# A third token tile of full height, earlier FFN rows, another order of the first transfers, and a second norm with one power: a hybrid decoder layer on one core

## The chip, the core and the metric

The kernel runs on one core of one Trainium2 chip. A core has five engines that run side by side, each through its own instructions in order: TensorE (PE in the profile; PEld is its weight load) multiplies matrices into PSUM, VectorE (DVE) and ScalarE (ACT) do elementwise work, GpSimd (POOL) does small elementwise work and issues transfers, and SyncE (SP) issues transfers. Sixteen DMA engines move the data. Engines wait for each other by semaphores.

The metric is the device time of one launch in microseconds; lower is better. The profile is of one execution. Its times count from the start of the span, which is the time from the program's first instruction to its last.

## What is computed

One step of a decoder layer, on 256 prompt tokens (one sequence, states zero) and 64 sample tokens (8 sequences of 8 tokens, with states given). All 320 tokens go through the layer together; model width D = 2048.

```
u = x @ w_in                                  # q k v o i f z xbc dt: 4096 + 8 + 2560 + 16 columns
h_m = mlstm(q, k, v, o, i, f)                 # 4 heads of 256; matrix memory C, normaliser n, running max m
h_s = ssd(z, conv4(xbc), dt)                  # 16 heads of 64, state 64 x 128, two B/C groups
x = layer_norm1(2**0.25 * x + concat(h_m, h_s) @ w_out)
up = x @ w_up                                 # 2 x 5504 columns
c = conv3(up)                                 # depthwise over tokens; the two rows before come from state_ffn_conv
x = layer_norm2(2**0.25 * x + (silu(c_gate) * c_value) @ w_down)
```

`layer_norm` is (x - mean) * rsqrt(var + 1e-5) * g + b. The outputs are y for prompt and sample, and all new states. Everything is float32.

## The kernel before

**Layout.** Activations lie with features in the 128 partitions and the 320 tokens along the free axis: columns 0 to 255 are the prompt, 256 to 319 the sample. A big product is made as three matmuls on split operands: each weight and each activation is split into a rounded part `hi` (a ScalarE copy, L74) and a rest `lo` (a VectorE subtraction, L75), and hi x hi, hi x lo and lo x hi are added in PSUM. `run_groups` (L262) goes over output units of 128 features, in quarters of 4 k-tiles; each quarter is 12 matmuls of 320 columns. `Stream` loads the weights on SyncE's queue (the first two tiles on ScalarE's, L61) into four buffers of 512 KB and splits them four quarters ahead.

**Order.** The main stream is: w_in in 52 units, w_out in 16, then three rounds of w_up and w_down. Everything else is background work in generators (`Tasks`, L116). A task's `yield n` means: not again before the planner's clock has moved n ns. That clock is a sum of estimated matmul and transpose times (`mm`, `transpose`, L227 to 238), so it follows the order of PE's instructions and not real time. `run_groups` steps the tasks after each quarter (`pump`, L285). What a task emits takes its place in each engine's program order there. `wait(flag)` holds a task, not an engine; the engines wait only for data.

**Token tiles.** Where tokens must lie in partitions (a transpose, or a product that contracts over tokens) the kernel works in three tiles: tokens 0 to 127, 128 to 255, and the 64 sample tokens as a tile of 64 partitions (`tok`, L249). So many PE instructions are 64 rows high or 64 columns wide: the transposes of x (L410 to 412), of the mLSTM heads (L1253), the row broadcasts (`diag3`, `colbc`, L313 to 325), the scores and their products.

**The sample's state term.** For SSD and mLSTM the sample's output is a product with the step's own tokens plus a product with the old state. The state products of four sequences land in four 32-partition strips of one bank, 8 rows used in each (L833 and L1173). They are scaled into a tile `yi`, and a product with the selection matrix `sel` (L906 and L1227) takes the eight rows of each strip to the right tokens and adds them.

**First transfers** (L435 to 444, L392): SyncE issues x columns 0 to 255, the identity, the sample's first 512 columns, and then the rest; the first two weight tiles go out on ScalarE's queue. `x_transpose` (L402) makes `XH`, `XL` for 128 features from two prompt tiles and one sample tile. `load_small` (L462) issues some 17 small loads on GpSimd. `keep_x` (L416) adds XH and XL again for the gates.

**FFN rows.** `ffn_consts` (L1339) starts with the second w_out group; after `yield 25000` it issues ten loads of old conv rows and conv weights on GpSimd, after `yield 20000` more it transposes them on PE (L1350, L1356).

**The second norm.** `down_task` (L1530) adds the last product, transposes each 128 features to tokens-in-partitions and takes their statistics (`bn_stats`, L1549); `times_g` (L1558) multiplies them with g. After the last unit (L1618 to 1661) the 16 statistics are aggregated, the reciprocal root is made by a ScalarE root, a VectorE reciprocal and a refinement, the row terms are transposed, and 12 products of 5 rows bring b - mean * rs * g; VectorE (tiles 0 and 1) or ScalarE and GpSimd (the sample) add them, and SyncE stores.

Of the kernel before, what the change touches and what calls it, by code (L numbers as in the profile page):

```python
# [13 lines left out]
NT = 320  # L14
# [7 lines left out]
class Stream:  # L22
# [21 lines left out]
    def load(self, upto=None, own=()):  # L44

        own = list(own)
        while self.nr < len(self.raws) and (own or self.live < self.RB):
# [12 lines left out]
            for c in range(0, m, step):  # L60
                (self.nc.sync if self.nr > 1 else self.nc.scalar).dma_start(t[:, :, c:c + step], src[:, :, c:c + step])  # L61
# [109 lines left out]
def _hybrid_step(ctx, tc, I, O):  # L171
# [77 lines left out]
    def tok(i):  # L249
        return 128 if i < 2 else 64  # L250
# [3 lines left out]
    sel = cp.tile([128, 2, 64], F32, name="sel")  # L254
# [58 lines left out]
    def diag3(dg, cols_of):  # L313
        for i in range(3):
            n = tok(i)
            V.tensor_scalar(dg[0:n, i, 0:n], ident[0:n, 0:n], cols_of(i)[0:n], None, ALU.mult)
        return dg

    def colbc(dg):

        ps = bank()
        for i in range(3):
            n = tok(i)
            mm(ps[:, 128 * i:128 * i + n], ones[0:n, :], dg[0:n, i, 0:n], True, True)
        return ps
# [75 lines left out]

    def x_transpose(c, kks=range(4)):  # L402
# [4 lines left out]
        for kk in kks:  # L407
# [27 lines left out]
    xs_in = mt("T10", [64, D])  # L435
    for c in range(4):
        x_load(c)
        s = slice(512 * c, 512 * c + 512)
        dma(xs_in[:, s], I["x_sample"].rearrange("b t f -> (b t) f")[:, s])
        if c == 0:  # L440
            src = I["x_prompt"][0, :, 256:512].rearrange("(i p) f -> p i f", p=128)
            dma(box["x", 0][:, :, 256:512], src)
            own = [mt("T4", [128, 1024]) for _ in range(4)]
        st.load(2 * c + 2, (own[0:2], own[2:4], (), ())[c])
# [16 lines left out]

    def load_small():  # L462
# [14 lines left out]
        hr = mt("T10", [24, 1536])  # L477
        gdma(hr, I["state_ssm_conv"][0].rearrange("b r c -> (b r) c"))
        gdma(c_tm, I["c_tm"])
        gdma(dsk, I["ssm_D"].broadcast_to([128, 16]))  # L480
        gdma(m01, I["c_m01"])
        gdma(sel, I["c_sel"])
# [5 lines left out]
        for i in range(12):  # L488
            transpose(ps[:, 24 * i:24 * i + 24], hr[:, 128 * i:128 * i + 128])
        A.activation(histx, ps[:, 0:288].rearrange("p (a b) -> p a b", b=24), AF.Copy)  # L490
# [20 lines left out]
    def gate_task(pg):  # L511
        gf, gi = mt("T2", [128, 384]), mt("T2", [4, NT])
        V.memset(gf[:, NT:384], 0.0)
        V.tensor_copy(gf[:, 0:NT], pg[:, 0:NT])
# [5 lines left out]
        for i in range(3):  # L520
            mm(pt[:, 24 * i:24 * i + 24], gf[:, 128 * i:128 * i + 128], fold[:, 0:24], True, True)
        pf = bank()
        mm(pf[0:4, 0:NT], fold[:, 0:4], gf[:, 0:NT], True, True)
# [36 lines left out]
        transpose(pd[0:48, 0:64], dt3[0:64, 2, :])  # L560
# [4 lines left out]
        V.tensor_copy(dtf[32:48], pd[32:48, 0:64])  # L565
# [47 lines left out]
        for i in range(3):  # L613
            transpose(p1[:, 128 * i:128 * i + 128], T1[:, 128 * i:128 * i + 128])
        A.activation(TT1, p1[:, 0:384].rearrange("p (a b) -> p a b", b=128), AF.Copy)
        p2 = bank()
# [59 lines left out]
    def ssd_cb():  # L676
# [4 lines left out]
        for g in range(2):  # L681
# [3 lines left out]
            mm(ps[0:64, 384:448], B[:, g, 256:NT], C[:, g, 256:NT], True, True)  # L685
            t = mt("T2", [128, 448])
            G.memset(t[64:128, 384:448], 0.0)
            V.tensor_tensor(t[:, 0:384], ps[:, 0:384], m01[:, 0:384], ALU.mult)
            V.tensor_tensor(t[0:64, 384:448], ps[0:64, 384:448], m01[0:64, 384:448], ALU.mult)
# [76 lines left out]
    def ssd_xdt():  # L766
# [3 lines left out]
        for i in range(3):  # L770
            n = tok(i)
            for hh in range(2):
                ps = bank()
                for j in range(4):
                    transpose(ps[0:n, 128 * j:128 * j + 128], XS[:, 4 * hh + j, 128 * i:128 * i + n])
                V.tensor_tensor(by(xdt[0:n, i, 512 * hh:512 * hh + 512], 64), by(ps[0:n, :], 64),
                                bcl(dt3[0:n, i, 32 + 8 * hh:40 + 8 * hh], 64), ALU.mult)
                yield 500
        box["xdt"] = xdt
        flags.add("xdt")  # L780

    def ssd_sample():
# [22 lines left out]
        yield from wait("x4")  # L805
        yi = {}
        for b in range(8):
# [19 lines left out]
            if b % 4 == 3:  # L827
                x = b // 4
                for g in range(2):
# [6 lines left out]
                    yi[g, x] = y  # L836
# [5 lines left out]
        box["yi"] = yi  # L842
# [5 lines left out]
    def ssd_heads():  # L848
# [41 lines left out]
        for j in range(8):  # L890
# [47 lines left out]
    def ssd_norm():  # L938
        var = sm([128, 3, 2])
        G.memset(var, 1.0)  # L940
        for g in range(2):
# [10 lines left out]
            for i in range(3):  # L952
                mm(ps[0:tok(i), 2 * i:2 * i + 2], sq[:, 128 * i:128 * i + tok(i)], ones[:, 0:2], True, True)
            pv = ps[:, 0:6].rearrange("p (a b) -> p a b", b=2)
            V.tensor_scalar(var[:, 0:2, g], pv[:, 0:2, 0], 1.0 / 512, None, ALU.mult)
            V.tensor_scalar(var[0:64, 2:3, g], ps[0:64, 4:5], 1.0 / 512, None, ALU.mult)
# [769 lines left out]
```

## Time and profile before

| | |
|---|---|
| median of 3 runs | 1579.27 us (1578.6 to 1581.3) |
| the profiled execution | 1580.12 us, of it the span 1578.3 us |
| TensorE clock granted, mean over the execution | 0.992 |
| data moved by DMA | 253.97 MB, mean 161 GB/s |
| weight stream, first matmul | at 8.83 us |
| last output product to span's end | 1566.4 to 1578.3 us |

The page has the busy time of each engine, the span in 40 slices, the DMA queues, the chain of work that ended last, and groups of instructions. A group's row reads: line, engine, operation, out<-in, shape, xcount, then busy us and mean ns of one, then the idle time of the engine just before them. A row of the timeline reads: start and duration in us, engine, line, operation, out<-in, shape, count of instructions merged into it. `128*64` before a shape is the part of the array used: rows times columns. A PE product of float32 operands shows as two instructions. In the windows view a row has the stretch, its length, busy time and count of each engine (PE, PEld, DVE, ACT, POOL), the granted clock, the DMA engines' share and GB/s. PE's matmuls overlap, so the time that one takes is read from start to start.

### The profile page before, as it was taken

How to read it: one execution, taken by the hardware profiler on the slowest of the kernel's cores; microseconds unless marked ns; L12 is line 12 of the kernel's file. 1: busy time of each engine (PE TensorE's matmuls, PEld its weight loads, DVE VectorE, ACT ScalarE, POOL GpSimd, SP SyncE). 2: the span in 40 equal slices, each digit the busy share in tenths (PEclk: the TensorE clock that was granted, in tenths of full speed). 3: DMA queues.
4: the chain of work that ended last, by engine and by line, in shares of the span. 5: the costliest groups of instructions: out<-in, count | busy, mean ns of one | idle time of the engine just before them, and what ended most of it. 6: DMA issues, size and time to landing. Idle time of an engine off the chain costs nothing.

```text
span 1578.3 us, 27987 instructions
## 1 busy us (share of the span) xinstructions
PE 1553.8 (98%) x10547; PEld 1502.5 (95%) x10547; DVE 976.6 (62%) x1957; ACT 773.1 (49%) x1532; POOL 290.3 (18%) x601
## 2 busy tenths in 40 slices
PE   9999999999999997999999999999999999999997
PEld 7999999998889997999999999999999999999996
DVE  5775445656677585687777545565644465556765
ACT  3665433435445453476666435555533455555332
POOL 4213220024311073133321000000000000001301
PEclk9999999999999998999999999999999999999998
DMA  9456665577665566445554455455444545455642
GB/s 260 147 161 160 187 187 172 143 193 208 195 221 183 169 183 138 134 147 149 149 151 135 157 158 146 148 156 152 136 152 144 167 145 151 143 154 168 170 140 79
DMA packets 267080, 253.97 MB, mean 161 GB/s; under 512 B 18804, under 2 KB 261263, under 8 KB 266816
## 3 DMA queue, kind: packets, MB, share of 16 engines
q1 hardware_dynamic: 260432, 246.76, 53.2%
q0 software_dynamic: 4928, 4.37, 1.3%
q8 instruction: 82, 1.34, 0.3%
q10 hardware_dynamic: 1584, 1.05, 0.3%
q14 instruction: 54, 0.44, 0.1%
HBM read 231.63 MB, written 20.43 MB: 160 GB/s over the span
## 4 chain that ended last, share of the span: by engine, by line
PE 86%; issue 7%; DMA 2%; POOL 1%; DVE 1%; ACT 1%; POOLq 0%; SPq 0%; DVEq 0%; ACTq 0%
PE bk L232 84%; PE bk L238 2%; DMA rows<-ffn_conv_w 1%; POOL T L425 1%; DMA raw<-w_out 1%; DVE lo L75 1%; DMA T<-ln_g 0%; DMA gbias<-ssm_dt_bias 0%; DMA xT<-T 0%; POOL big L1654 0%; ACT hi L74 0%; DVE big L1393 0%; DVE big L1389 0%; ACT L657 0%; ACT T L644 0%
## 5 line engine op out<-in xcount | busy, mean ns | idle before, releaser
L75 DVE TENSOR_TENSOR lo<-raw,hi 128x512 fp32r<-128x512 f32 (+2 forms) x800 | 556.4, 706 | 391.7 <-ACT hi L74 389.3
L74 ACT ACTIVATE hi<-raw 128x512 fp32r<-128x512 f32 (+2 forms) x800 | 486.3, 616 | 455.9 <-PE bk L232 427.3
L232 PE MATMUL bk<-big,hi 128*128 128x320 f32 (+1 forms) x2752 | 609.3, 310 | 0.0
L232 PEld LDWEIGHTS bk<-big,hi 128*128 128x128 f32 x2752 | 462.2, 188 | 0.1
L232 PE MATMUL bk<-big,lo 128*128 128x320 f32 (+1 forms) x1376 | 426.5, 310 | 0.0
L232 PE MATMUL bk<-XH,hi 128*128 128x320 f32 x832 | 270.2, 325 | 0.1
L232 PEld LDWEIGHTS bk<-big,lo 128*128 128x128 f32 x1376 | 259.3, 188 | 0.0
L232 PE MATMUL bk<-XH,lo 128*128 128x320 f32 x832 | 258.2, 310 | 0.1
L232 PE MATMUL bk<-XL,hi 128*128 128x320 f32 x832 | 258.0, 310 | 0.0
L232 PE MATMUL bk<-HH,hi 128*128 128x320 f32 x688 | 214.2, 311 | 0.0
L232 PE MATMUL bk<-HH,lo 128*128 128x320 f32 x688 | 212.6, 309 | 0.0
L232 PE MATMUL bk<-HL,hi 128*128 128x320 f32 x688 | 212.5, 309 | 0.0
L232 PEld LDWEIGHTS bk<-XH,hi 128*128 128x128 f32 x832 | 157.2, 189 | 14.7 <-issue 5.5
L232 PEld LDWEIGHTS bk<-XL,hi 128*128 128x128 f32 x832 | 157.4, 189 | 0.4
L232 PEld LDWEIGHTS bk<-XH,lo 128*128 128x128 f32 x832 | 157.2, 189 | 0.6 <-DVE lo L75 0.6
L1492 DVE SCALAR_TENSOR_TENSOR c<-c,fcol,c 128x336 f32<-128x336 f32 x172 | 98.0, 570 | 58.6 <-ACT c L1490 55.6
L232 PEld LDWEIGHTS bk<-HL,hi 128*128 128x128 f32 x688 | 129.2, 188 | 0.0
L232 PEld LDWEIGHTS bk<-HH,hi 128*128 128x128 f32 x688 | 129.2, 188 | 0.0
L232 PEld LDWEIGHTS bk<-HH,lo 128*128 128x128 f32 x688 | 129.1, 188 | 0.0
L193 POOL TENSOR_SCALAR fst<-c 128x18 f32<-128x18 f32 x86 | 22.2, 265 | 567.4 <-ACT c L1485 567.4
L232 PE MATMUL bk<-MH,hi 128*128 128x320 f32 x256 | 80.9, 316 | 0.0
L232 PE MATMUL bk<-MH,lo 128*128 128x320 f32 x256 | 80.1, 313 | 0.7 <-DVE lo L75 0.7
(338 smaller groups left out, 1505.8 us busy)
## 6 DMA issues: line engine op xcount, KB each, us to landing
raw<-ffn_w_up SPq DMA_DIRECT2D x172, 512.0 KB, 3.8
raw<-w_in SPq DMA_DIRECT2D x100, 512.0 KB, 4.1
raw<-ffn_w_down SPq DMA_DIRECT2D x71, 512.0 KB, 3.6
raw<-w_out SPq DMA_DIRECT2D x32, 512.0 KB, 3.9
T<-state_mlstm_C SPq DMA_DIRECT2D x32, 256.0 KB, 5.8
s_C<-T SPq DMA_DIRECT2D x32, 256.0 KB, 4.9
T<-state_ssm SPq DMA_DIRECT2D x8, 512.0 KB, 6.5
s_ssm<-T SPq DMA_DIRECT2D x8, 512.0 KB, 5.3
```

The costliest lines, as they stand in the source:

```text
L74: nc.scalar.activation(h, src, AF.Copy)
L75: nc.vector.tensor_tensor(l, src, h.bitcast(F32), ALU.subtract)
L193: G.tensor_scalar(out, in_, 1.0, 0.0, ALU.mult, ALU.add)
L232: nc.tensor.matmul(out, lhsT=lhsT, rhs=rhs, start=start, stop=stop)
L238: nc.tensor.transpose(out, in_, ident[b:b + p, b:b + p])
L425: G.tensor_tensor(t, f32(XH(k, 2)), f32(XL(k, 2)), ALU.add)
L1492: V.scalar_tensor_tensor(c[:, 0:336], xp[:, j:j + 336], fcol[:, j, i:i + 1], c[:, 0:336], ALU.mult, ALU.add)
```

## The change

1. The third token tile is columns 192 to 319, full height, with the sample in its upper half: `TS` takes the place of `tok`. Transposes, broadcasts, scores and their products take 128 rows or columns; results are used in partitions 64 to 127.
2. The lower half of that tile (rows 0 to 63) carries the state term. Four small GpSimd transfers (`gather`) take the eight rows of each strip of `yi` to rows 0 to 63 of the third tile of `xdt` or `VT`, and the matrix that multiplies the tile has the identity in these rows. The products with `sel` go, as does `sel`.
3. The state of a pair of SSD heads is made in two halves of 64 columns.
4. The sample's x is loaded as 128 x 1024, so that one 128x128 transpose serves features k and k + 8; the conv rows as 96 x 384, in three transposes.
5. First transfers: the identity and the sample's first 256 columns of each half go out on ScalarE's queue; all weights go out on SyncE's, in another order.
6. `ffn_consts`: the yields become 12000 and 40000.
7. Second norm: the first 15 statistics are aggregated early, the last aggregate goes over three triples; one power on GpSimd makes the reciprocal root; six products into an unused bank stand in front of the transposes; one copy in place of three; the sample's stores are issued by GpSimd, each after its addition, and the sample comes second of the three tiles.

```diff
-                (self.nc.sync if self.nr > 1 else self.nc.scalar).dma_start(t[:, :, c:c + step], src[:, :, c:c + step])
+                self.nc.sync.dma_start(t[:, :, c:c + step], src[:, :, c:c + step])
...
-    def tok(i):
-        return 128 if i < 2 else 64
+    TS = (slice(0, 128), slice(128, 256), slice(192, NT))
...
-            mm(ps[:, 128 * i:128 * i + n], ones[0:n, :], dg[0:n, i, 0:n], True, True)
+        for i in range(2):
+            mm(ps[:, TS[i]], ones, dg[:, i, :], True, True)
+        mm(ps[:, 256:NT], ones, dg[:, 2, 64:128], True, True)
...
-    for _ in range(7):
+    for _ in range(9):
         mm(warm[:, 0:128], ones, ones, True, True)
...
-            dma(ident, I["c_ident"])
+            nc.scalar.dma_start(ident, I["c_ident"])
...
-            transpose(ps[:, 256:NT], xs_in[:, 128 * k:128 * k + 128])
-            A.activation(XH(k), ps[:, 0:NT], AF.Copy)
-            V.tensor_tensor(XL(k), ps[:, 0:NT], f32(XH(k)), ALU.subtract)
+            parts = [(k, 0, 256)]
+            if k < 8:
+                transpose(ps[:, 256:384], xs_in[:, 128 * k:128 * k + 128])
+                parts = [(k, 0, NT), (k + 8, NT, 384)]
+            parts = [(kx, slice(256 if a else 0, 256 if b == 256 else NT), ps[:, a:b]) for kx, a, b in parts]
+            for kx, o, src in parts:
+                A.activation(XH(kx)[:, o], src, AF.Copy)
+            for kx, o, src in parts:
+                V.tensor_tensor(XL(kx)[:, o], src, f32(XH(kx))[:, o], ALU.subtract)
...
+    def xs_load(eng, a, b):
+        for e in range(2):
+            eng.dma_start(xs_in[64 * e:64 * e + 64, a:b], xs_src[:, 1024 * e + a:1024 * e + b])
+
+    x_load(0)
+    xs_load(nc.scalar, 0, 256)
+    own = [mt("T4", [128, 1024]) for _ in range(4)]
+    st.load(1, own[0:1])
+    dma(box["x", 0][:, :, 256:512], I["x_prompt"][0, :, 256:512].rearrange("(i p) f -> p i f", p=128))
+    xs_load(nc.sync, 256, 512)
+    st.load(2, own[1:2])
+    x_load(1)
...
+    def swapped(out, in_):
+        for e in range(2):
+            gdma(out[64 * e:64 * e + 64], in_[64 - 64 * e:128 - 64 * e])
...
+    def gather(out, y):
+        for c in range(4):
+            gdma(out[8 * c:8 * c + 8], y[32 * c:32 * c + 8])
...
-        yield from wait("x4")
+        yield from wait("x4", "xdt")
...
-                    yi[g, x] = y
+                    gather(box["xdt"][32 * x:32 * x + 32, 2, 512 * g:512 * g + 512], y)
...
-            for x in range(2):
-                mm(ps[:, 256:NT], box["yi"][g, x][:, 128 * (j % 4):128 * (j % 4) + 128], sel[:, x, :], x == 0, False)
             for e, (p, f) in enumerate(pe):
-                mm(ps[p, 256:NT], xdt[0:64, 2, f], mw[e][0:64, 384:448], False, True)
+                mm(ps[p, 256:NT], xdt[:, 2, f], mw[e][:, 384:448], True, True)
             for i in range(2):
-                mm(po, xw[:, i, :], btok[:, i, g, :], i == 0, i == 1)
+                for e, (p, f) in enumerate(pe):
+                    mm(po[p, :], xw[:, i, p], btok[:, i, g, :], i == 0, i == 1)
...
-                box["yi", h, x] = yi
+                gather(box["VT"][32 * x:32 * x + 32, 2, h, 0:257], yi[:, 0:257])
...
-        mm(ps[0:64, 0:257], P[0:64, 384:448], VT[0:64, 2, h, 0:257], True, False)
-        for x in range(2):
-            mm(ps[0:64, 0:257], sel[:, x, :], box.pop(("yi", h, x))[:, 0:257], False, x == 1)
-        A.activation(num[0:64, 2, 0:257], ps[0:64, 0:257], AF.Copy)
+        mm(ps[:, 0:258], P[:, 384:512], VT[:, 2, h, :], True, True)
+        A.activation(num[:, 2, :], ps[:, 0:258], AF.Copy)
...
     def ffn_consts():
-        yield 25000
+        yield 12000
...
-        yield 20000
+        yield 40000
...
-            for i in range(3):
-                t = slice(128 * i, 128 * i + tok(i))
+            for t in (slice(0, 128), slice(128, NT)):
                 V.tensor_tensor(a[:, t], a[:, t], ps[:, t], ALU.add)
...
+            V.bn_stats(lnst[:, i, m, :] if m < 15 else agg[:, i, 3:9], pt[:, 128 * i:128 * i + 128])
         if m == 14:
-            A.activation(fin["sd"], fin["eps"], AF.Sqrt)
+            for i in range(3):
+                V.bn_aggr(amv[:, i, :], lnst[:, i, :, :])
+            V.tensor_copy(agg[:, :, 1], amv[:, :, 0])
+            V.tensor_scalar(agg[:, :, 2], amv[:, :, 1], 1920.0, 2048.0 * LN_EPS, ALU.mult, ALU.add)
...
-        V.bn_aggr(mv[0:tok(i), i, :], lnst[0:tok(i), i, :, :])
-    A.activation(fin["sd"], mv[:, :, 1], AF.Sqrt, bias=fin["eps"][:, 0:1])
-    V.tensor_scalar(var, mv[:, :, 1], LN_EPS, None, ALU.add)
-    V.reciprocal(rs, fin["sd"])
-    V.tensor_tensor(u, rs, rs, ALU.mult)
-    V.tensor_tensor(u, u, var, ALU.mult)
-    V.tensor_scalar(var, u, 0.375, -1.25, ALU.mult, ALU.add)
-    V.tensor_tensor(u, u, var, ALU.mult)
-    V.scalar_tensor_tensor(rs, u, 1.875, rs, ALU.add, ALU.mult)
+        V.bn_aggr(mv[:, i, :], agg[:, i, :])
+    G.tensor_tensor(rs, mv[:, :, 1], nhalf, ALU.pow)
...
+    warm = bank()
+    for _ in range(6):
+        mm(warm[:, 0:256], ones, fin["g"][:, 0:256], True, True)
     ps = bank()
     for i in range(3):
-        transpose(ps[0:5, 128 * i:128 * i + tok(i)], f32(nbc[0:tok(i), i, :]))
-    for i in range(3):
-        t = slice(128 * i, 128 * i + tok(i))
-        V.tensor_copy(nbr[:, t], ps[0:5, t])
+        transpose(ps[0:5, 128 * i:128 * i + 128], f32(nbc[:, i, :]))
     times_g(15, fin["pt"])
+    V.tensor_copy(nbr, ps[0:5, 0:384])
...
-        for i in range(3):
+        for i in (0, 2, 1):
...
                 G.tensor_tensor(t, t, w2, ALU.add)
+                gdma(ys[:, s], t)
...
-        if c:
-            dma(*late)
-        late = ys[:, s], fin["r2"][:, s]
-    dma(*late)
```

More of the change, by code (lines that the diff above doesn't have):

```diff
@@ L314, in diag3 @@
         for i in range(3):
-            n = tok(i)
-            V.tensor_scalar(dg[0:n, i, 0:n], ident[0:n, 0:n], cols_of(i)[0:n], None, ALU.mult)
+            V.tensor_scalar(dg[:, i, :], ident, cols_of(i), None, ALU.mult)
         return dg
@@ L433, in keep_x @@
         yield from gate_task(pg)
[L435 to L444, printed above, removed]
+    xs_in = mt("T10", [128, 1024])
+    xs_src = I["x_sample"].rearrange("b t f -> (b t) f")
+    def xs_load(eng, a, b):
[9 more added lines that the diff above has]
+    x_load(1)
+    st.load(3, own[2:3])
+    xs_load(nc.sync, 512, 1024)
+    st.load(4, own[3:4])
+    x_load(2)
+    st.load(6)
+    x_load(3)
+    st.load(8)
     gw = mt("T2", [128, 16, 32])
@@ L476, in load_small @@
         gdma(m0, I["state_mlstm_m"][0].rearrange("b h -> h b"))
-        hr = mt("T10", [24, 1536])
-        gdma(hr, I["state_ssm_conv"][0].rearrange("b r c -> (b r) c"))
-        gdma(c_tm, I["c_tm"])
+        hr = mt("T2", [96, 384])
+        for q in range(4):
+            gdma(hr[24 * q:24 * q + 24], I["state_ssm_conv"][0].rearrange("b r c -> (b r) c")[:, 384 * q:384 * q + 384])
+        swapped(c_tm[:, 2, :], I["c_tm"][:, 2, :])
+        gdma(c_tm[:, 0:2, :], I["c_tm"][:, 0:2, :])
         gdma(dsk, I["ssm_D"].broadcast_to([128, 16]))
-        gdma(m01, I["c_m01"])
-        gdma(sel, I["c_sel"])
+        gdma(m01[:, 0:384], I["c_m01"][:, 0:384])
+        swapped(m01[:, 384:448], I["c_m01"][:, 384:448])
         yield 17000
@@ L487, in load_small @@
         ps = bank()
-        for i in range(12):
-            transpose(ps[:, 24 * i:24 * i + 24], hr[:, 128 * i:128 * i + 128])
-        A.activation(histx, ps[:, 0:288].rearrange("p (a b) -> p a b", b=24), AF.Copy)
+        for a in range(3):
+            transpose(ps[:, 96 * a:96 * a + 96], hr[:, 128 * a:128 * a + 128])
+        A.activation(histx.rearrange("p (q a) b -> p a q b", a=3), ps[:, 0:288].rearrange("p (a q b) -> p a q b", a=3, b=24),
+                     AF.Copy)
         d2 = dsk.rearrange("p (j e) -> p j e", e=2)
@@ L559, in gate_task @@
         pd = bank()
-        transpose(pd[0:48, 0:64], dt3[0:64, 2, :])
+        transpose(pd[0:48, 0:128], dt3[:, 2, :])
         V.tensor_copy(Bf[:, 0:NT], pb[0:48, 0:NT])
@@ L613, in gate_task @@
         for i in range(3):
-            transpose(p1[:, 128 * i:128 * i + 128], T1[:, 128 * i:128 * i + 128])
+            transpose(p1[:, 128 * i:128 * i + 128], T1[:, TS[i]])
         A.activation(TT1, p1[:, 0:384].rearrange("p (a b) -> p a b", b=128), AF.Copy)
+        G.memset(TT1[0:64, 2, 32:48], -BIG)
+        G.memset(TT1[0:64, 2, 64:68], 1.0)
         p2 = bank()
@@ L774, in ssd_xdt @@
                 for j in range(4):
-                    transpose(ps[0:n, 128 * j:128 * j + 128], XS[:, 4 * hh + j, 128 * i:128 * i + n])
-                V.tensor_tensor(by(xdt[0:n, i, 512 * hh:512 * hh + 512], 64), by(ps[0:n, :], 64),
-                                bcl(dt3[0:n, i, 32 + 8 * hh:40 + 8 * hh], 64), ALU.mult)
+                    transpose(ps[:, 128 * j:128 * j + 128], XS[:, 4 * hh + j, TS[i]])
+                V.tensor_tensor(by(xdt[p, i, 512 * hh:512 * hh + 512], 64), by(ps[p, :], 64),
+                                bcl(dt3[p, i, 32 + 8 * hh:40 + 8 * hh], 64), ALU.mult)
                 yield 500
@@ L1251, in ml_out @@
             ps = bank()
-            for i in range(3):
-                transpose(ps[:, 128 * i:128 * i + tok(i)], num[0:tok(i), i, 128 * e:128 * e + 128])
+            for i in (2, 0, 1):
+                transpose(ps[:, TS[i]], num[:, i, 128 * e:128 * e + 128])
             A.activation(Q[:, 2 * h + e, :], ps[:, 0:NT], AF.Copy, scale=col(C_NM + 2 * h + e))
@@ L1512, in _hybrid_step @@
     fin = {}
-    lnst = fsm([128, 3, 16, 6])
+    lnst, agg, amv = fsm([128, 3, 15, 6]), fsm([128, 3, 9]), fsm([128, 3, 2])
     def fstate():
@@ L1644, in _hybrid_step @@
         s = slice(512 * c, 512 * c + 512)
[L1645 to L1646 removed]
+        for i in (0, 2, 1):
             t = fin["r2"][:, s] if i == 2 else fin["r01"][:, i, s]
[L1648 to L1649 removed]
+            w = bank()
+            mm(w, nbr[:, 128 * i:128 * i + 128], fin["rows"][:, s], True, True)
             if i == 2:
[L1651 to L1653 removed]
+                A.activation(t, t, AF.Copy, scale=rs[64:128, i:i + 1])
+                w2 = fr("rx", [128, 512])[64:128]
+                A.activation(w2, w[64:128, :], AF.Copy)
                 G.tensor_tensor(t, t, w2, ALU.add)
+                gdma(ys[:, s], t)
             else:
[L1656 removed]
+                V.scalar_tensor_tensor(t, t, rs[:, i:i + 1], w, ALU.mult, ALU.add)
                 dma(O["y_prompt"][0, 128 * i:128 * i + 128, s], t)
[L1658 to L1661 removed]
 _INS = ["x_prompt", "x_sample", "state_mlstm_C", "state_mlstm_n", "state_mlstm_m", "state_ssm", "state_ssm_conv",
```

88 lines of the change are left out of this document (34 added, 54 removed).

## The prediction, made before the changed kernel was timed

> **What bounds the kernel now.** I read the page first (busy time of each engine), then TensorE's list of waits, then the chain of waits.
>
> ```profile
> PE 1553.8 (98%) x10547; PEld 1502.5 (95%) x10547; DVE 976.6 (62%) x1957; ACT 773.1 (49%) x1532; POOL 290.3 (18%) x601
> ```
> ```profile
> PE bk L238 <- DMA rows<-ffn_conv_w: 8.3, 1, 8.3
> PE bk L238 <- DVE fsm L1634: 4.5, 1, 4.5
> PE bk L238 <- DMA T<-x_sample: 1.3, 1, 1.3
> ```
> ```profile
> 152.86 1.75 PE bk L238 x16
> ```
> ```profile
> 630.89 825.17 PE bk L232 x5604
> ```
> TensorE (PE) is the bound. It waits three times for anything of size: for the FFN's conv rows, for the chain of small operations of the second norm, and at the start. Everywhere else it issues back to back: 825.17 / 5604 = 0.147 us a matmul in the stream that the change leaves alone, 1.75 / 16 = 0.109 us a full 128x128 transpose. So whatever takes PE time out of the stages before the FFN shortens the run one to one, as long as VectorE and ScalarE, which split the weights ahead, keep up.
>
> **The FFN rows.** First the rows load's issue on GpSimd (POOL), then stretches of the windows view: length, busy us of PE, PEld, DVE, ACT and POOL with counts, granted clock, DMA share, GB/s.
>
> ```profile
> 576.06 12.80 POOL L1343 DMA_DIRECT2D rows<-state_ffn_conv  x8
> ```
> ```profile
> 546.00:560.00 14.00, 13.08 (x86) 12.58 (x86) 11.65 (x22) 6.50 (x13) 2.57 (x4) 1.00 0.63 208
> 560.00:576.00 16.00, 16.00 (x111) 16.00 (x110) 14.88 (x22) 10.46 (x21) 10.05 (x10) 1.00 0.40 126
> 576.00:590.00 14.00, 14.00 (x97) 14.00 (x96) 10.82 (x20) 6.80 (x12) 14.00 (x10) 1.00 0.87 187
> 590.00:602.00 12.00, 3.83 (x27) 3.56 (x25) 4.85 (x2) 1.78 (x3) 6.48 (x8) 0.79 1.23 196
> 602.00:612.00 10.00, 9.91 (x55) 9.90 (x56) 5.65 (x10) 3.90 (x8) 2.44 (x3) 0.74 0.26 82
> ```
> The load is issued at 576 into a stretch where the DMA engines are over-full (0.87, then 1.23), and PE, in order, stands 8.3 us before the transposes of these rows. Then it runs at a mean clock of 0.74 for 10 us, which loses (1 - 0.74) x 10 = 2.6 us more. Both go: 10.9 us. The first yield falls from 25000 to 12000 of the planner's ns, so the issue moves some 13 us or more forward, to between 552 and 563, and the transposes move 7000 back. The load, 26 us from its issue to 602, then has over 35 us. The rows now share the DMA engines with weight loads at shares of 0.63 and 0.40, with room. On POOL the ten issues, about 15 us, stand ahead of the sums of squares (L1400, L1403), which only the first norm needs, after the last group. VectorE is busy 14.88 of 16 us there, so splits may come late: 0 to 2 us lost. If the cover fails, the whole 10.9 stays.
>
> **PE shapes.** Timeline, TensorE only: start, duration, shape. I take start to start, since durations overlap.
>
> ```profile
> 19.02 2.30 PE L238 MATMUL bk<-ident,T 128*128 128x128 f32 x12
> 21.25 0.41 PE L232 MATMUL bk<-XH,hi 128*128 128x320 f32 x1
> ```
> ```profile
> 254.51 0.87 PE L232 MATMUL bk<-T,T 128*64 128x256 f32 x8
> 255.31 0.66 PE L232 MATMUL bk<-sel,T 128*128 128x64 f32 x4
> 255.90 0.97 PE L232 MATMUL bk<-T,T 64*64 64x64 f32 x8
> 256.62 0.39 PE L232 MATMUL bk<-XH,hi 128*128 128x320 f32 x1
> ```
> ```profile
> 355.13 1.04 PE L238 MATMUL bk<-ident,T 128*128 128x128 f32 x8
> 356.00 1.04 PE L232 MATMUL bk<-T,T 128*128 128x258 f32 x4
> 356.68 0.50 PE L232 MATMUL bk<-XH,hi 128*128 128x320 f32 x1
> ```
> ```profile
> 387.30 0.65 PE L232 MATMUL bk<-T,T 64*64 64x257 f32 x2
> 387.87 1.08 PE L232 MATMUL bk<-T,sel 128*64 128x257 f32 x4
> 388.88 0.42 PE L232 MATMUL bk<-XH,hi 128*128 128x320 f32 x1
> ```
> ```profile
> 492.25 1.15 PE L238 MATMUL bk<-ident,T 128*128 128x128 f32 x6
> 493.33 0.42 PE L232 MATMUL bk<-XH,hi 128*128 128x320 f32 x1
> ```
> Merged rows hide the 64-row transposes, but the spacing shows them. Eight full transposes take 356.00 - 355.13 = 0.87 us, 0.109 each; the six of one head, two of them 64 rows high, take 1.08 where 0.65 would do: 0.21 for each small one, on the way in and out.
> - x, slices 1 to 3: twelve in 2.23 us (eight full, four small). Slice 1 becomes twelve full (1.31), slices 2 and 3 eight (0.87): 0.92 + 2 x 1.36 = 3.6 us. The twelve conv-row transposes become three: 0.5, an estimate from 0.109 each.
> - Transposes of the heads: 4 x (1.08 - 0.65) = 1.7.
> - SSD, per pair of heads: 254.51 to 256.62 is 2.11 us. The first eight (0.80) stay, less a shape change (0.1); the four `sel` go; the third tile costs two pairs of 64 columns, the state four pairs of 128. The first eight move 768 columns in pairs, about 1 ns each, so 640 columns cost about 0.65. 2.11 - (0.70 + 0.65) = 0.75; eight times, 6.0. If the halves did not run side by side, the state would cost as much again and the gain would be near 0.2 each, 1.6 in all.
> - mLSTM output: 387.30 to 388.88 is 1.58 us and becomes one product, half of the four in 0.68: 0.34. With the stream's slow first matmul behind it I take 1.3; four heads, 5.2.
> - A dozen other small shapes (scores, CB, four row broadcasts, norm sums, dt) at the same 0.2: 2.4, between 1 and 3.5.
>
> Sum 19.4. The column-narrow outputs that become full (down, v, xdt) I cost at nothing: their transposes already fill the same spacing. Where VectorE lags (the pairs of heads), a faster PE may meet a late split: minus 0.7.
>
> **GpSimd work that comes instead.** Twelve gathers of four small DMAs replace the `sel` products. One issue takes 0.58, and PE's last state product of a head's inputs comes 15 us before the output product:
>
> ```profile
> 372.11 1.08 PE L232 MATMUL bk<-T,T 128*32 128x257 f32 x16
> ```
> ```profile
> 432.75 0.58 POOL L1129 DMA_DIRECT2D s_n<-T  x1
> ```
> ```profile
> rows<-state_ffn_conv POOLq DMA_DIRECT2D x8, 86.0 KB, 11.4
> ```
> Four issues, 2.3 us, and at worst the 11.4 us from issue to landing of the conv rows, with many more and in the fullest stretch: 13.7, just inside 15. The issuing POOL waits for the product's scaled copy, and behind it queue the copies that spread k and v and fill the next head's query block; VectorE and PE want these some us later. For SSD the gathers end two states before the first pair of heads. Nothing is charged. The state loop's new wait for `xdt` holds that task alone, and `xdt` starts on the same flags as the operand that it waited for before. The memsets and identity copies go to POOL, 18% busy.
>
> ```profile
> 32.57 0.75 PE L232 MATMUL bk<-T,T 128*32 128x320 f32 x8
> ```
> The small loads grow from 17 to 23 issues, 3.5 us; behind them stand the additions of `keep_x`, whose first product PE takes at 32.57, when 23 issues (13 us, and some waits for landings) are long past.
>
> **The start.**
>
> ```profile
> 8.83 0.64 PE L232 MATMUL bk<-XH,hi 128*128 128x320 f32 x1
> ```
> ```profile
> 11.28 0.47 PE L232 MATMUL bk<-XL,hi 128*128 128x320 f32 x1
> 11.54 0.47 PE L232 MATMUL bk<-XH,lo 128*128 128x320 f32 x1
> ```
> The first matmul stands at 8.83, after the 1.3 us wait for x_sample. Identity and sample now go out on ScalarE's queue while SyncE issues x and then the first weights, so the sample no longer stands fifth in line. The second weight tile moves behind the rest of x on SyncE; it is wanted by the third unit only, after 24 matmuls, over 6 us later. I take the 1.3 us wait as gone and charge 0.2 for the sample's second, smaller split, which now stands ahead of the weights' split (a small operation takes 0.17 in the tail below): 1.1 earlier. Each of the next three small transposes costs 0.4 less (0.21 at half clock): 2.3 in all. But matmuls stand 0.26 apart here (11.28, 11.54) and 0.147 in the stream: half clock. If the clock rises at the same moment, 2.3 us at half speed are worth 1.2. Bounds -1 and +3.5. The Trainium skill's "TensorE: Matmul & The Clock Gate" (Part 1, the HAM clock gate) says that the clock rises after one busy window of about 3.4 us: by it the work packed denser could lift the clock one window earlier, worth another 1.7 us, or 2.9 in place of 1.2; by the trace I can't place the windows.
>
> **The tail.**
>
> ```profile
> 1561.36 1.45 DVE L1623 BATCH_NORM_AGGREGATE fsm<-fsm 128x2 f32<-128x96 f32 x3
> ```
> ```profile
> 1564.45 0.16 DVE L1632 SCALAR_TENSOR_TENSOR fsm<-fsm,fsm 128x3 f32<-128x3 f32 x1
> ```
> ```profile
> 1564.92 0.17 DVE L1634 TENSOR_TENSOR fsm<-fsm,fsm 128x3 fp32r<-128x3 f32 x1
> ```
> ```profile
> 1567.21 5.36 DVE L1656 SCALAR_TENSOR_TENSOR big<-big,fsm,bk 128x512 f32<-128x512 f32 x8
> ```
> ```profile
> 1568.74 5.15 POOL L1654 TENSOR_TENSOR big<-big,rx 64x512 f32<-64x512 f32 x4 [93.32 <-ACT rx L1653]
> ```
> ```profile
> L1234 DVE BATCH_NORM_AGGREGATE sm<-sm 128x2 f32<-128x6 f32 x12 | 2.2, 182 | 0.4
> ```
> ```profile
> L193 POOL TENSOR_SCALAR T<-n0f 128x4 f32<-128x4 f32 x16 | 4.4, 290 | 13.1 <-ACT n0f L1013 10.5 <-DMA s_C<-T 2.5
> ```
> Three aggregates over 9 instead of 96 numbers cost 3 x 0.2: 0.8 saved. From their end (1562.81) to 1564.45 stand root, reciprocal and refinement, 1.6 us; one power replaces them. No power is in the trace: I take 0.4, the 0.29 of POOL's four-element operation with a hand-over each way; bounds 0.2 and 1.3 (POOL's 1.29 for each of the four additions). 1.2 saved. From 1565.09 to the first output at 1567.21 there are 2.1 us; one copy in place of three, the multiplication moved beside the transposes, and six warming matmuls (PE idles there) save 0.5, and one addition fewer 0.1. Output therefore starts 2.6 earlier. Then POOL's four additions (5.15) get four issues of 0.58 between them, 7.5 us, which ends later than the stores did on SyncE: I keep 2.3, bounds 0 and 4.
>
> **The sum.** 10.9 + 19.4 - 0.7 + 1.2 + 2.3 = 33.1. The profiled execution took 1580.1 (span 1578.3 and 1.8 around it): 1547.0. The median of the runs shown is 0.9 below that execution, so 1546.
>
> **Rivals.**
> - The FFN wait stays in another form (rows still late, or weights starved by them): 10.9 back, 1557. Against: 35 us for 26, idle DMA engines at 560. Chance 0.08.
> - The shapes give half (the pairs of halves run one after the other, small shapes cost nothing): 9 back, 1555. Against: the 0.87 against 1.08 above. Chance 0.05.
> - The power is slow: at 1.3 in place of 0.4 the tail keeps 1.4: 1547. The Trainium skill's "GPSIMD Engine Reference" (2.1, Instruction dispatch) speaks against the change: the first call of a freshly loaded kernel pays about 6 us for its code; by that the tail would lose 3.3 instead of winning 2.3, 1552. No run here shows it. Chance 0.07.
> - Slower than before: the gathers queue in order on POOL behind work that waits, and PE stands before the output products of four heads and the first pair of heads. The point is the 15 us: a gather that lands later stops PE. Priced as the FFN wait, 5 x 10.9 = 54.5 less the 33 won: about 1601; it beats the gain from 6.6 us per wait. For it: 48 new issues. Against: POOL is 18% busy. Chance 0.04.
>
> **How the numbers follow.** The forecast has 0.76, 1540 to 1552. The range takes in slow power, lost FFN gain and half shapes on one side, and early clock and full small shapes on the other: 1538 to 1558. About 0.2%, 3 us, is what a measurement tells from no change. Faster 0.94, same 0.02, slower 0.04.
>
> **What would show it.** TensorE's waits without ffn_conv_w, full clock at 602 to 612; no 64-row transposes, the pair of heads in about 1.35 us and the mLSTM output in 0.35; first matmul near 7.7; the power near 0.3 us and the first output 3.4 us after the aggregates start. Wrong if PE waits on a gather, on `raw`, or on splits near the SSD heads for more than a few us in all.

## The result: 1559.3 us, 1.3% faster, 13 us above the forecast

The changed kernel takes 1559.33 us (median of 4 runs, 1557.03 to 1562.0), the kernel before 1579.24 us in the runs beside it. The ratio is 0.9872, with a 95% interval of 0.9853 to 0.9891. So 19.9 us are won where 33 were forecast, and the time lies above the range. The profiled execution took 1562.0 us; its span went from 1578.3 to 1560.0 us, 18.3 us.

The page's row of engines in the changed kernel has 18.6 us less of TensorE and 33 us more of GpSimd:

```profile
PE 1535.2 (98%) x10530; PEld 1497.2 (96%) x10530; DVE 977.9 (63%) x1955; ACT 771.7 (49%) x1537; POOL 323.1 (21%) x667
```

TensorE's list of waits there (engine, line, what it waited for: us in all, times, the longest):

```profile
PE bk L232 <- DVE lo L75: 5.0, 3, 3.1
PE bk L232 <- DMA T<-w_in: 2.9, 1, 2.9
PE bk L238 <- DMA T<-x_sample: 1.6, 1, 1.6
...
PE bk L238 <- DVE fsm L1652: 0.2, 1, 0.2
```

The two waits that the change was to remove are gone: none for the FFN rows, 0.2 us in place of 4.5 for the second norm. Two others have come: 5.0 us for `lo` splits (0.7 before) and 2.9 us for a load of `w_in` columns that was in no row of the list before.

Where the time went shows best when the same matmul is looked up in both traces. The table does that for the first matmul of some weight quarters (all 808 are in the same order in all kernels). "Three edits" is the kernel of the experiment "The three edits together". "x rows read back" are the residual rows that `keep_x` stores and `load_rx` loads again for the additions of `out_task` (L1402).

| weight quarter, and what lies behind it | before, us | changed, us | won | three edits, us | won |
|---|---|---|---|---|---|
| 7: start and two x slices | 30.62 | 26.73 | 3.9 | 26.60 | 4.0 |
| 9: first gate product | 35.10 | 35.73 | -0.6 | 31.19 | 3.9 |
| 137: pairs of SSD heads | 321.93 | 314.23 | 7.7 | 309.68 | 12.3 |
| 209: mLSTM | 512.12 | 496.11 | 16.0 | 491.54 | 20.6 |
| 230: x rows read back | 551.43 | 538.17 | 13.3 | 531.99 | 19.4 |
| 247: the burst on GpSimd | 581.35 | 574.50 | 6.9 | 561.91 | 19.4 |
| 256: the old wait for the FFN rows | 608.57 | 590.33 | 18.2 | 577.75 | 30.8 |
| last weight matmul | 1559.38 | 1541.20 | 18.2 | 1528.63 | 30.8 |
| end of span | 1578.3 | 1560.0 | 18.3 | 1546.2 | 32.1 |

**What came as predicted.** Timeline of TensorE in the changed kernel, one pair of SSD heads, one mLSTM output, one set of head transposes:

```profile
252.77 1.42 PE L232 MATMUL bk<-T,T 128*64 128x256 f32 x20
254.12 0.42 PE L232 MATMUL bk<-XH,hi 128*128 128x320 f32 x1
...
379.49 0.60 PE L232 MATMUL bk<-T,T 128*128 128x258 f32 x2
379.74 0.50 PE L232 MATMUL bk<-XH,hi 128*128 128x320 f32 x1
...
481.38 0.82 PE L238 MATMUL bk<-ident,T 128*128 128x128 f32 x6
481.95 0.39 PE L232 MATMUL bk<-XH,hi 128*128 128x320 f32 x1
```

Start to start, the pair takes 254.12 - 252.77 = 1.35 us (forecast 1.35), the output 0.25 (0.34), the six transposes 0.57 (0.65). From quarter 9 to 209 the kernel wins 16.6 us where the parts of the forecast that lie there give 16.4.

**The start.** TensorE at its first products and around the first gate product:

```profile
6.67 0.63 PE L238 MATMUL bk<-ident,T 128*128 128x128 f32 x4 [1.57 <-DMA T<-x_sample]
8.27 0.63 PE L232 MATMUL bk<-XH,hi 128*128 128x320 f32 x1 [0.97 <-ACT hi L74]
...
28.42 0.31 PE L232 MATMUL bk<-XH,lo 128*128 128x320 f32 x1
31.64 1.27 PE L232 MATMUL bk<-T,T 128*32 128x320 f32 x8 [2.91 <-DMA T<-w_in]
32.84 0.64 PE L232 MATMUL bk<-XH,hi 128*128 128x320 f32 x1
33.27 0.47 PE L232 MATMUL bk<-XL,hi 128*128 128x320 f32 x1
33.54 0.47 PE L232 MATMUL bk<-XH,lo 128*128 128x320 f32 x1
```

The wait for `x_sample` is still there, and the first matmul stands at 8.27, 0.6 us earlier than before. The gate product (31.64) waits for its other operand, the gate columns of `w_in` (`gw`). They land at 31.50, hardly earlier than before the change (32.01), and there TensorE arrived at 32.57, just behind the landing. The 3.9 us won by then end in this wait, and the matmuls behind it stand 0.27 apart: half clock.

**The FFN stretch.** VectorE, then GpSimd:

```profile
554.21 0.49 DVE L1402 SCALAR_TENSOR_TENSOR big<-rx,bk 128x320 f32<-128x320 f32 x1
554.73 4.70 DVE L1415 TENSOR_TENSOR big<-big,c 128x320 f32<-128x320 f32 x2
559.35 2.71 DVE L1419 SCALAR_TENSOR_TENSOR big<-big,cols,big 128x320 fp32r<-128x320 f32 x1
561.98 0.68 DVE L75 TENSOR_TENSOR lo<-raw,hi 128x512 fp32r<-128x512 f32 x1
```
```profile
538.04 0.46 POOL L193 TENSOR_SCALAR c<-big 128x320 f32<-128x320 f32 x1 [38.51 <-DVE big L1415]
538.65 12.70 POOL L1369 DMA_DIRECT2D rows<-state_ffn_conv  x8 [0.15 <-issue]
...
553.78 0.98 POOL L1426 TENSOR_TENSOR c<-c,big 128x320 f32<-128x320 f32 x1
554.73 0.86 POOL L1429 TENSOR_TENSOR c<-c,c 128x320 f32<-128x320 f32 x1
...
560.84 0.86 POOL L1426 TENSOR_TENSOR c<-c,big 128x320 f32<-128x320 f32 x1
564.68 1.16 POOL L1429 TENSOR_TENSOR c<-c,c 128x320 f32<-128x320 f32 x1 [2.98 <-ACT c L1428]
```

GpSimd issues row loads from 538.65 to 553.76. The first norm's sums wait behind them and then run in one burst, nine additions without a gap from 553.78 to 561.70. In that time VectorE finishes three operations in 7.3 us that take about 0.5 each elsewhere, and the split behind them starts only when the burst is over. TensorE, by the starts of its matmuls, stands 1.4 us at 561.2 and 3.3 us at 566.2.

```profile
554.00:562.00 8.00, 7.50 (x52) 7.24 (x50) 7.92 (x6) 2.28 (x4) 7.70 (x9) 1.00 0.98 147
562.00:571.00 9.00, 5.15 (x33) 4.89 (x34) 8.90 (x15) 4.25 (x9) 4.34 (x5) 1.00 0.24 77
571.00:575.00 4.00, 4.00 (x19) 4.00 (x18) 2.35 (x5) 1.14 (x2) 0.00 (x0) 0.57 0.78 250
```

The windows of the same stretch: VectorE is "busy" 7.92 of 8 us with six instructions, and after the waits the clock is 0.57 for 4 us.

**The tail.** Power, aggregates, first output, GpSimd's additions and stores:

```profile
1543.25 0.32 DVE L1648 BATCH_NORM_AGGREGATE fsm<-fsm 128x2 f32<-128x9 f32 x3
...
1547.01 5.36 DVE L1675 SCALAR_TENSOR_TENSOR big<-big,fsm,bk 128x512 f32<-128x512 f32 x8 [0.59 <-PE bk L232]
```
```profile
1543.71 0.89 POOL L1649 TENSOR_TENSOR fsm<-fsm,fsm 128x3 f32<-128x3 f32 x1 [86.50 <-DVE fsm L1648]
1547.98 1.27 POOL L1672 TENSOR_TENSOR big<-big,rx 64x512 f32<-64x512 f32 x1 [3.38 <-ACT rx L1671]
1549.55 0.62 POOL L1673 DMA_DIRECT2D y_sample<-big  x1 [0.30 <-POOL big L1672]
1550.19 1.28 POOL L1672 TENSOR_TENSOR big<-big,rx 64x512 f32<-64x512 f32 x1
```

The power takes 0.89 us. The first output starts 5.8 us after the last weight matmul instead of 7.8: 2.0 of the forecast 2.6 are won. But an addition, a pause and an issue repeat every 2.15 us on GpSimd, the last store is issued at 1556.06 and lands at 1558.38, and from the last weight matmul to the end of the span it is 18.75 us, nearly as long as before (18.95).

### The profile page after: what moved, and what is told of

It is laid out like the page before. It is cut to its first block, busy times and chain, and to the rows that moved or that the text cites. A ratio compares the mean times of both kernels' runs of the same rounds, so it can differ in the third digit from the quotient of the medians.

```text
span 1560.0 us, 28115 instructions
## 1 busy us (share of the span) xinstructions
PE 1535.2 (98%) x10530; PEld 1497.2 (96%) x10530; DVE 977.9 (63%) x1955; ACT 771.7 (49%) x1537; POOL 323.1 (21%) x667
## 4 chain that ended last, share of the span: by engine, by line
PE 95%; DMA 2%; DVE 1%; SPq 1%; POOL 0%; issue 0%; ACT 0%; POOLq 0%; ACTq 0%; DVEq 0%
PE bk L232 93%; PE bk L238 2%; DMA T<-w_in 1%; DMA rx<-xT 0%; SPq L61 0%; POOL big L1672 0%; DVE big L1415 0%; DVE lo L75 0%; DMA T<-x_sample 0%; DVE big L1419 0%; SPq L466 0%; DVE big L1402 0%; DVE big L1432 0%; POOL fsm L1649 0%; DVE big L1433 0%
## 5 line engine op out<-in xcount | busy, mean ns | idle before, releaser
L75 DVE TENSOR_TENSOR lo<-raw,hi 128x512 fp32r<-128x512 f32 (+2 forms) x800 | 552.2, 700 | 391.3 <-ACT hi L74 389.2
L193 POOL TENSOR_SCALAR fst<-c 128x18 f32<-128x18 f32 x86 | 22.1, 264 | 567.6 <-ACT c L1508 567.6
```

What stands on the lines that cost most here:

```text
L75: nc.vector.tensor_tensor(l, src, h.bitcast(F32), ALU.subtract)
L193: G.tensor_scalar(out, in_, 1.0, 0.0, ALU.mult, ALU.add)
```

## The experiments

Theory after the result: three losses. The gate weights land late (4.5 us with the half clock behind it); GpSimd's burst holds up VectorE (6 us with the half clock); the stores on GpSimd use up what the shorter chain wins (2 us). Rivals: the DMA engines are full at the start anyway; the rows' bytes starve the weights (the four `w_out` tiles issued from 540 to 556 land after a median of 11.2 us; the same four took 4.1 before); VectorE is simply full.

### Gate weights earlier

```diff
     x_load(3)
-    st.load(8)
     gw = mt("T2", [128, 16, 32])
...
     dma(gw[:, :, 8:24], w[:, :, 6664:6680])
+    st.load(8)
```

> The changed kernel with the two loads of the gate weights (8 and 16 columns of w_in) issued ahead of the weight tiles 6 and 7 instead of behind them; nothing else. Theory: the gain of the x transposes is made (the matched matmul of the 8th weight quarter stands 3.9 us earlier than before the change) and is lost at once, because the first gate product (31.64 us) waits 3.1 us for the gate weights' landing (31.50) and the clock is half for 3.4 us behind the wait, 1.4 us more. Then the loads land near 27 us, PE does not wait, the clock stays full, and the lead of 3.9 us is kept: -4 us, about 1555, and the matmuls from quarter 12 on stand 4 us earlier than in the changed kernel. Rival: the DMA engines are full in the first 30 us, tiles 6 and 7 now land some 3 us later and PE waits for their splits instead: 1559, the wait only changes its name.

1554.17 us (1553.11 to 1557.87), ratio 0.9848 [0.9833, 0.9863], 5.2 below the changed kernel. In its timeline the gate product starts at 29.28:

```profile
29.28 0.74 PE L232 MATMUL bk<-T,T 128*32 128x320 f32 x8 [0.82 <-DMA T<-w_in]
```

The wait is 0.8 in place of 2.9, there is no half clock behind it, and from quarter 9 on the matmuls stand 3.9 us earlier than in the changed kernel. Tiles 6 and 7 landed 3.8 and 3.7 us later (31.07 and 32.59) and nothing waited for them. The theory holds; the rival falls. The 5.2 of the medians is the less certain figure: the slowest of these runs lies inside the range of the changed kernel.

### Row loads spread out

```diff
             gdma(hr[:, 2 * b:2 * b + 2, :], ...)
+            yield 3000
...
+        yield 3000
         gdma(wr[:, 3, :], ...)
-        yield 40000
+        yield 13000
```

> The changed kernel with the ten loads of the FFN rows issued one by one, 3000 of the planner's ns apart, instead of all at once; the transposes of the rows stay where they are. The sums of the first norm on GpSimd then stand between the issues and do not pile up behind them. Theory A (the pile of sums, released in one burst at 553.8, holds up VectorE): VectorE's operations stay under 1 us each between 550 and 570, both waits for the lo splits (1.4 and 3.3 us) and the half clock behind them (1.4 us) go: -6 us, 1553. Theory B (the rows' bytes starve the weights: tiles land after 10 to 12 us instead of 4): the same bytes at half the rate, tiles land after 5 to 8 us, and most of the 6 us goes too. Theory C (VectorE is simply full in this stretch): no change, 1559.

1553.71 us (1553.28 to 1554.17), ratio 0.9841 [0.9826, 0.9855]: -5.6. C falls. TensorE still waits 2.0 us for `lo`, and VectorE's operations in this stretch still take up to 1.4 us where two or three additions fall beside them, so the miss is in "under 1 us each". This run can't tell A from B; the next one can.

### Sums later

```diff
         else:
+            if m < 9:
+                yield 20000
             e.tensor_tensor(s1, s1, d, ALU.add)
```

> The changed kernel with the sums of the first norm of features 1 to 8 put off by 20000 of the planner's ns; the row loads stay as they are, all at once. Theory A (the burst of sums behind the row issues holds up VectorE): VectorE's subtractions near 554 to 562 take 0.5 to 0.6 us in place of 2.4 and 2.7, the two waits for lo splits shrink from 4.7 us to under 1.5 us: -4 to -6 us, 1553 to 1555. Theory B (the rows' bytes starve the weights): tiles still land after 10 to 12 us and the splits are as late as they were: 1559. Theory C (VectorE is full): 1559 too, with VectorE busy over 95% from 552 to 564.

1553.61 us (1553.25 to 1553.9), ratio 0.9841 [0.9824, 0.9857]: -5.7. VectorE's subtractions in this run (durations in ns: least, median, most), and the DMA view for 538 to 555 us (KB each, median us to landing):

```profile
L1415 DVE TENSOR_TENSOR big<-big,c x5: 479/486/525, 546.0 to 555.4; 128x320 f32<-128x320 f32 x5
```
```profile
raw<-w_out SPq DMA_DIRECT2D x5, 512.0 KB, 13.1
```

The weight tiles land even later than in the changed kernel (13.1 against 11.2 us), and yet TensorE waits for `lo` 0.5 us in all. So A holds, and B and C fall: the slow tiles cost lead, not time. ScalarE's squares move with the sums here; the last experiment moves nothing but GpSimd.

### Sample stores on SyncE

```diff
-                gdma(ys[:, s], t)
...
+        if c:
+            dma(*late)
+        late = ys[:, s], fin["r2"][:, s]
+    dma(*late)
```

> The changed kernel with the sample's four stores issued on SyncE, one column block late, as they were before the change; nothing else. Theory: the end is set by GpSimd, which does add (1.28), a pause (0.3) and a store's issue (0.57) four times, 2.15 us apart. With the stores on SyncE the four additions follow each other in 5.2 us, the last store lands near 1556.7 in place of 1558.4, and the span's end follows the last landing by 0.9 in place of 1.6 us: -2 to -2.5 us, 1557. Rival: the prompt's stores (last landing 1556.75) and the landings' own 3 to 4 us set the end anyway: -1 us or less, 1558.5 or more.

1557.75 us (1555.53 to 1559.19), ratio 0.9865 [0.985, 0.988]: -1.6, less than the runs of either kernel differ among themselves. The profile is sharper: from the last weight matmul to the last landing 16.2 us (17.2 in the changed kernel, 18.0 before), to the end of the span 17.9 (18.75 and 18.95). GpSimd's four additions follow each other:

```profile
1542.61 4.96 POOL L1672 TENSOR_TENSOR big<-big,rx 64x512 f32<-64x512 f32 x4 [3.38 <-ACT rx L1671]
```

So the chain on GpSimd did set the last landing, but only 0.8 us reach the end: the span ends 1.7 us behind the last landing, where I expected 0.9. The other traces of this case say more. In all six with the sample's stores on GpSimd, GpSimd's first drain (an instruction at the program's end) ends 0.8 us behind the last landing, and from the last weight matmul to the span's end it is 18.7 to 19.1 us. In the four with the new chain and the stores on SyncE, that drain ends over 3 us ahead of the landing, and it is 17.6 to 17.9 us. So the stores on SyncE are worth about 1 us, and the late drain fits the longer end of the changed kernel. Why 1.7 us remain in this profile (1.3 in the three others) stays open.

### The three edits together, and two more

> The changed kernel with three edits together: gate weights loaded ahead of weight tiles 6 and 7, the sums of the first norm of features 1 to 8 put off by 20000 of the planner's ns, the sample's stores on SyncE. Theory: the three losses lie in different places and each was measured alone (1554.2, 1553.6, 1557.8 against 1559.3), so they add: 1559.3 - 5.1 - 5.7 - 1.6 = 1546.9, which is the forecast of 1546 made good, and shows that nothing else of size was lost. Rival: a TensorE that is earlier by 10 us meets another late transfer (xT rows at 520, weights), and the sum stays above 1550.

1548.75 us (1546.86 to 1549.92), ratio 0.9809 [0.9795, 0.9822]. The three edits win 10.6 of the 12.5 us that they win singly, 1.9 short of the sum; the rival's 1550 is not reached. The table above shows the losses of quarters 9 and 247 gone; that of quarter 230 is down from 2.7 to 1.2 us. TensorE's longest waits are now small. Three are at the start; "issue" and `lo` stand at the x rows read back (526.9 and 528.7 us):

```profile
PE bk L238 <- DMA T<-x_sample: 1.9, 1, 1.9
PE bk L232 <- issue: 1.1, 1, 1.1
PE bk L232 <- POOL ones L385: 1.0, 1, 1.0
PE bk L232 <- ACT hi L74: 1.0, 1, 1.0
PE bk L232 <- DVE lo L75: 0.7, 1, 0.7
```

Next to these, the gate weights ahead of `x_load(3)` and a later column-sum product (`out_task`, m = 0):

```diff
-            yield 5000
+            yield 8000
             pk = bank()
```

> As the three edits together, with the gate weights one place earlier still (ahead of the last slice of x) and the column-sum product of the first w_out unit put 3000 of the planner's ns later, so that it no longer stands on the landing of the x rows read back. Theory: the 0.8 us that TensorE still waits for the gate weights goes, and with it the wait of up to 1.3 us near 530 and the half clock behind it (1.5 us) in the runs that have it: 1544 to 1546. Rival: the later product delays the subtractions and their splits behind it, or the last slice of x lands late: 1547 or more.

1549.99 us (1548.49 to 1550.21), ratio 0.9815 [0.9802, 0.9828]: no better. The wait for the gate weights, which it was to remove too, no longer shows among the waits of the three edits. The product's wait became a wait for a split:

```profile
528.45 0.41 PE L232 MATMUL bk<-MH,lo 128*128 128x320 f32 x1 [2.54 <-DVE lo L75]
...
530.26 1.27 PE L232 MATMUL bk<-big,ones 128*128 128x320 f32 x2
```

VectorE stands in order before the addition that needs the x rows, with the splits behind it; moving TensorE's product doesn't help. Putting that addition off instead, beside the three edits:

```diff
+        if m < 4:
+            yield 4000
         x = rx[m // 4][:, m % 4, :]
```

> The three edits together, and the first four residual additions of w_out put 4000 of the planner's ns later, so that VectorE, which works in order, makes three lo splits before it waits for the x rows read back (landing near 527). Theory: in some executions these rows land a microsecond later, TensorE then waits for the column-sum product or for the lo splits queued behind the addition, and pays half clock besides, 3 us in all; without that the runs lie closer together and the median falls by 1 to 2 us: 1547 or 1547.5. Rival: the four later additions queue up with what follows on VectorE, or the PSUM banks come free late, and the time stays at 1548.8 or rises.

1547.96 us (1546.77 to 1548.45), ratio 0.9795 [0.9779, 0.9812]. It is the lowest median, but its interval overlaps with that of the three edits; the 1 to 2 us are not shown. Both beat both kernels. The edit also did more than was meant: GpSimd's copy of the first sum (L193), which stood ahead of the row loads, now came behind them, so the loads were issued at 501.0 in place of 533.0 with the three edits alone, and the x rows landed 11.1 us after their issue in place of 7.2. This run is therefore no clean trial of its theory.

### One part undone, one part alone

In the changed kernel the yields of `ffn_consts` set back to 25000 and 20000; then in the kernel before only these two changed to 12000 and 40000.

> The changed kernel with the two yields of the FFN rows as before the change (25000 and 20000), everything else changed. Theory: the earlier rows removed a wait of 10.9 us and brought back 4.7 us of waits for splits and 1.4 us of half clock, so undoing them costs 3 to 5 us: 1562 to 1564, with a wait for ffn_conv_w near 8 us. Rival: the earlier rows bought nothing in the changed kernel (the profiled execution keeps only 2.2 us of them): 1559 to 1560.

> The kernel before with the two yields of the FFN rows alone changed (12000 and 40000). Theory: the burst of sums behind the issues holds up VectorE here too, so of 10.9 us only 4 to 7 are won: 1572 to 1575, with a wait for lo splits near 575 to 585. Rival: the burst hurts only together with the other parts of the change, and all 10.9 are won: 1568.

Undone: 1562.59 us (1562.3 to 1564.66), ratio 0.99 [0.9886, 0.9913], with 7.9 us of waiting for ffn_conv_w: the move is worth 3.3 us. Alone: 1574.75 us (1573.39 to 1575.93), ratio 0.9973 [0.9962, 0.9985], 4.1 us below the kernel before, with 4.9 us of waiting for `lo`. So the burst comes with the move itself, in either kernel, and 3 to 4 of its 10.9 us are left.

### One more addition on GpSimd

```diff
             e.tensor_tensor(s2, s2, q, ALU.add)
+            if m < 9:
+                G.tensor_tensor(extra, d, q, ALU.add)
```

> The changed kernel with one more GpSimd addition of the same size (128x320, two operands in SBUF, into a scratch tile that nothing reads) behind each pair of sums of features 1 to 8; ScalarE, VectorE, the transfers and their order stay as they are. Theory A (GpSimd's additions hold up VectorE's operations on two SBUF operands): the burst behind the row issues grows from some 8 to 12 us, VectorE's subtractions and splits there are slow for longer, and TensorE's waits for lo splits grow from 4.7 to 7 to 10 us: 1562 to 1565. Rivals B and C (the rows' bytes, or VectorE's own load): GpSimd has room, no change, 1559.

1561.24 us (1560.13 to 1562.49), ratio 0.9883 [0.9864, 0.9902]: +1.9 by the medians, but the runs overlap with those of the changed kernel, so a longer time is not shown. What the trace shows is VectorE. Its subtractions in the changed kernel, then in this run:

```profile
L1415 DVE TENSOR_TENSOR big<-big,c x4: 487/856/3553, 550.1 to 563.1; 128x320 f32<-128x320 f32 x4
```
```profile
L1416 DVE TENSOR_TENSOR big<-big,c x3: 492/1851/8486, 551.8 to 563.5; 128x320 f32<-128x320 f32 x3
```

The burst, now 13 additions, runs from 551.3 to 561.7, and one subtraction takes 8.49 us in it. In the four traces with the burst of nine (the changed kernel, gate weights earlier, stores on SyncE, and the kernel before with the rows moved) VectorE's longest operation takes 3.54 to 3.56 us; in the seven where the burst is missing or broken up, at most 1.4 in the same quarters. Nothing but GpSimd's additions differs from the changed kernel here, so they are the cause of the long operations. TensorE loses no more than by the burst of nine: from quarter 230 to 247 it takes 37.4 us, those four 34.9 to 37.5, and 29.9 in five of the traces without the burst. The waits of 7 to 10 us that I expected did not come; there is one of 4.6.

## Why the prediction missed

- **FFN rows, 10.9: got 3.3.** The step that failed: the ten issues on POOL "stand ahead of the sums of squares (L1400, L1403), which only the first norm needs", with "0 to 2 us lost". I asked who waits for the sums, and nobody does. I did not ask what the sums do when they are let go together: between quarters 230 and 247 they cost 6.4 us (36.3 in place of 29.9). The wait itself went, and the rows' transposes do not wait. The issue stood at 538.65, about 552 in the time of before, at the early edge of the forecast 552 to 563; part of that is luck, since it was held there by GpSimd's copy at 538.04, which the forecast doesn't have. The "room" on the DMA engines was not there either (`w_out` tiles took 11.2 us in place of 4.1), but no time was lost by it. The rival "the FFN wait stays in another form" named late rows or starved weights; the form was a third one. Sums put off give back 5.7 us.
- **The start, 1.2, and x slices.** By quarter 7 the gain was 3.9 where start and two slices give 3.5. The slices gave 1.0 and 1.4 for 0.9 and 1.4, the start 1.4 for 1.2. But the start's number came out by other terms than its own, which is luck in part. "I take the 1.3 us wait as gone": it is 1.6 us, a wait of 1.0 us for the first weights' split follows it, and the first matmul stands 0.6 us earlier, not 1.1; but full clock came at 14.66 instead of 16.74. The step that failed and cost time: for `keep_x` I checked GpSimd's additions, "long past" at 32.57, and not the product's other operand, whose load landed 0.6 us ahead of that moment. Every microsecond won before it was lost in it: 4.5 with the half clock in the profile, 5.2 by the medians of the runs with the loads moved.
- **Tail, 2.3: got 0.2.** The chain is 2.0 shorter, not 2.6; the power took 0.89 where I took 0.4, inside its bounds. The step that failed: "7.5 us, which ends later than the stores did on SyncE: I keep 2.3". Additions, pauses and issues took 8.6 us, 0.3 us of pause each being left out, and the end came 1.6 instead of 0.9 us behind the last landing. The 6 us that the Trainium skill's "GPSIMD Engine Reference" (2.1, Instruction dispatch) gives for a first call do not show in the power.
- **Shapes, 19.4 - 0.7: right** within half a microsecond as a sum, pairs of halves and all; its small terms were not measured one by one. No product waits for a gather; the rival slower than before did not come near.
- **The x rows read back** are a loss that the forecast has no term for. The profiled execution loses 2.7 us more between quarters 209 and 230: the rows landed at 530.84, 7.3 us after their issue, TensorE waited 1.2 us for the column-sum product and 0.7 for a split, and half clock followed. This comes and goes. In the profiles of the gate weights earlier, the three edits and the rows undone the same rows landed 6.9 to 7.4 us after their issue, and the stretch took 0.9 to 1.3 us longer than before; in those of the spread rows, the later sums, the stores on SyncE and the added addition they landed after 5.1 to 5.8 us, and nothing was lost. So part of the miss of this one execution is chance; it lies 2.7 us above the median.

Together: 33.1 less the three shortfalls (7.6, 4.5 and 2.1) is 18.9; the medians won 19.9, the span of the profiled execution 18.3.

With the three edits the kernel stands 30.1 us below before, where the forecast had 33.

## What to carry to other kernels

When a stage gets faster, list every operand of the next few products with its landing time: one that landed half a microsecond early is the next wait. When work is put ahead of other work on an in-order engine, ask not only who needs the delayed work but what it does when it comes all at once. GpSimd additions on SBUF operands are cheap when strewn between VectorE's and dear in a row.

## What the hardware showed

**VectorE can stand still for a whole burst.** Its operations with two operands in SBUF (L1415, L1419, the splits of L75) took up to 3.56 us, in the last experiment 8.49, beside GpSimd additions of 0.7 to 1.2 us each; the one L1402 in the burst of the changed kernel (554.21), with one operand in PSUM, kept to 0.49. The Trainium skill's "SBUF — State Buffer" (Who interferes with whom) says that a VectorE instruction with two SBUF inputs contends with a GpSimd instruction that reads SBUF, and one with a single SBUF input does not: the trace agrees. It says that the loser waits for the whole instruction; here it waited for about ten of them.

**The clock gate works on a fixed grid.** In the changed kernel the half clock between 30 and 1540 us comes in stretches of 3.41 us, from 31.73, 533.49 and 571.03, whole multiples of 3.413 us apart. In all twelve traces, from where they record the clock to the last weight matmul, a window of that grid in which TensorE idled 1.86 us or more was followed by half clock, and one with 1.64 or less was not; a window at half clock with 0.44 us idle or more in it was followed by another, and one with 0.23 or less by full clock. So a wait of 2 us may cost 3.7 (itself and half of 3.41) and the same wait across two windows only itself. The Trainium skill's "TensorE: Matmul & The Clock Gate" (Part 1, the HAM clock gate) gives a free-running window of 3413 ns, which agrees, and one idle window for the drop; by these runs about half a window of idle time is enough.
